# Preparing the split weights of later stages during the feed-forward stages of a ten-stage transformer kernel

## The chip, the core and the metric

The kernel runs on one NeuronCore of a Trainium2 chip. Its time is the device time of one execution in microseconds, from three executions. A profiled execution gives the trace that is read here. The engines are TensorE (PE in the views, and PEld for its weight loads), VectorE (DVE), ScalarE (ACT), GpSimd (POOL) and SyncE (SP), whose queue issues all of this kernel's DMAs.

## The reference, cut to what matters

Two hybrid layers (each: feed-forward, mix, feed-forward) and one block of four branches with a last feed-forward follow each other, on 512 tokens of width 1024, in float32.

```python
def hybrid_layer(x, pos, ...):                      # twice, l = 0 and 1
    x = x + 0.5 * swiglu(rmsnorm(x, ffn1_norm), ffn1_w_gate, ffn1_w_up, ffn1_w_down)
    h = rmsnorm(x, mix_norm) @ w_in                 # the mix stage: three kinds of attention
    ...
    x = x + jnp.concatenate([o_a, o_b, o_c], axis=-1) @ w_out
    x = x + 0.5 * swiglu(rmsnorm(x, ffn2_norm), ffn2_w_gate, ffn2_w_up, ffn2_w_down)

# second_block: four branches of h = rms(x), each gated and projected
y_fox = _merge_heads(_fox_attention(fq, fk, fv, log_f))      # "fox"
y_lru = _rg_lru_branch(proj("lru_x"), proj("lru_g"), ...)    # the recurrence, "lru"
y_sb  = _merge_heads(_stick_breaking_attention(sq, sk, sv))  # stick-breaking, "sb"
y_mem = _merge_heads(_mem_attention(mq, mk, mv))             # "mem"
...
x = x + (jax.nn.silu(gate_pre) * val) @ w_down[l]            # the last feed-forward
```

## The kernel before

The stages run one after the other: ffn(1,0), mix 0, ffn(2,0), ffn(1,1), mix 1, ffn(2,1), mem, fox, lru, sb, the output projection, and the last feed-forward (`ffn2`). In `ffn(f, l)` f is 1 or 2 and l the layer.

Every product of float32 numbers is made of three matmuls on halves (`mm3`, lines 308 to 310): each operand is held as a rounded part and a remainder. For a weight the two parts are made on the chip when it is needed, by `weights`: a DMA brings the raw weight (`raw`, 2 buffers; line 289), ACT copies it into the rounded part (`wh`, 4 buffers; line 293), and the remainder (`wl`, 4 buffers) is subtracted on line 296, by DVE for one weight and by POOL for the next:

```python
WENG = ("av", "ap")
raw = self.wp.tile([P, 1024], FT, name="raw", bufs=2)
hi, sub = WENG[self.wc % len(WENG)]
self.wc += 1
(nc.vector if sub == "v" else nc.gpsimd).tensor_sub(lo[:, :n], raw[:, :n], h[:, :n].bitcast(FT))
```

There are two `raw` buffers and two entries in `WENG`, and both are taken in turn by the same calls, so one buffer's weights always go to DVE and the other's to POOL.

A feed-forward has two halves, of 12 and 10 hidden tiles. For each tile a gate and an up weight (512 KB each) give 24 matmuls apiece (`pd` and `pa`); sigmoid on ACT, products on DVE and POOL (line 408) and a split follow. Then eight down steps, each of two weights: 384 KB and 18 matmuls apiece in the first half ("down of 12"), 320 KB and 15 apiece in the second ("down of 10"), and DVE adds the result to `x` (line 420).

The mix stages, fox and sb are written as plans of steps (projections, heads); the tile framework's scheduler then orders the instructions of each engine, once, when the program is built. Each engine executes its list in that order, and so does SP with the DMAs: what stands behind a waiting instruction waits as well.

Of the kernel before, what the change touches and what calls it, by code (L numbers as in the profile page):

```python
# [17 lines left out]
FT = mybir.dt.float32  # L18
# [179 lines left out]
class Build:  # L198
    def __init__(self, ctx, tc, I):
        self.tc, self.nc, self.I = tc, tc.nc, I  # L200
        nc = self.nc
        e = ctx.enter_context
        self.hlp = e(tc.tile_pool(name="hlp", bufs=1))
        self.wp = e(tc.tile_pool(name="wp", bufs=3))
        self.xp = e(tc.tile_pool(name="xp", bufs=1))
        self.fp = e(tc.tile_pool(name="fp", bufs=7))
        self.sp = e(tc.tile_pool(name="sp", bufs=2))
        self.cp = e(tc.tile_pool(name="cp", bufs=1))
        self.np_ = e(tc.tile_pool(name="np_", bufs=1))
# [12 lines left out]
        self.spare = True  # L222

    def consts(self):
        nc = self.nc
# [54 lines left out]
                self.early.append(self.weights(first.pop(0), D))  # L280


    def weights(self, ap, n):

        nc = self.nc
        raw = self.wp.tile([P, 1024], FT, name="raw", bufs=2)
        h = self.wp.tile([P, 1024], FR, name="wh", bufs=4)
        lo = self.wp.tile([P, 1024], FR, name="wl", bufs=4)
        nc.sync.dma_start(raw[:, :n], ap)
        hi, sub = WENG[self.wc % len(WENG)]  # L290
        self.wc += 1
# [99 lines left out]

    def ffn(self, f, l):
        nc, I = self.nc, self.I
        hs, rb, _ = self.norm(f"ffn{f}_{l}")
        for half, (a, b) in enumerate(HALVES):
            hid = []
            for n in range(a, b):
                wg = self.early.pop(0) if self.early else self.weights(I[f"wg{f}_{l}"][n], D)
                pg = self.ps()
                self.proj(pg, wg, hs)  # L400
                wu = self.early.pop(0) if self.early else self.weights(I[f"wu{f}_{l}"][n], D)
                pu = self.ps("pa")
# [12 lines left out]
            for n in range(KD):
                po = self.ps()
                for q in range(2):
                    w = self.weights(wd[2 * n + q], kg * P)
                    self.proj(po, w, hid[q * kg:(q + 1) * kg], start=q == 0, stop=q == 1)
                nc.vector.scalar_tensor_tensor(self.x[n], po, 0.5, self.x[n], op0=OP.mult, op1=OP.add)  # L420


    def halves(self, src, scale=None):
# [170 lines left out]
    def mix(self, l):  # L594
        nc, I = self.nc, self.I
        hs, rb, rc = self.norm(f"mix_{l}", spill=True)
        ci, si, tk = (self.table(k) for k in (2, 3, 4))
        win = I[f"win_{l}"]

        def tile_of(n):  # L600
            w = self.weights(win[n], D)
            ps = self.ps()
            self.proj(ps, w, hs)
            return ps
# [91 lines left out]
            ckv.append(rkc)  # L696

        def values_a():
            wa = [self.weights(I[f"wav_{l}"][g], 768) for g in range(4)]
            va.extend(self.hl("v") for _ in range(3))  # L700
            self.tokens(hs, wa, 384, 2, 384, lambda t, p: self.values(p, va, t, rc[:, t:t + 1], A_H))

        def values_b():
            wb = [self.weights(I[f"wbv_{l}"][g], 640) for g in range(4)]
            vb.extend(self.hl("v") for _ in range(3))
            self.tokens(hs, wb, 320, 2, 320, lambda t, p: self.values(p, vb, t, rc[:, t:t + 1], B_H))

        def values_c():
            wv = self.weights(I[f"wuv_{l}"], 640)
# [14 lines left out]
        def dense_c(h):  # L724
            p, s = divmod(h, 2)
            if p not in kn:
                m = P if p < 2 else 64
                wkn = self.weights(I[f"wuk_{l}"][p], 256)
# [8 lines left out]
            w = self.weights(I[f"wuq_{l}"][h], 384)  # L737
            pq = self.ps()
            self.proj(pq, w, cq)
            f, g = self.f(), self.f("g")  # L740
# [159 lines left out]
        return self.stack_k(self.halves(f), tags=("qk", "e"))  # L900

    def vgroup(self, hs, name, grp, rc):
        w = [self.weights(self.I[name][2 * grp + q], 1024) for q in range(2)]
# [54 lines left out]
    def fox(self, hs, rb, rc):  # L958
# [2 lines left out]
        vs, qs, ks, ys, got = {}, {}, {}, [], []  # L961

        def forget(_):
            w = self.weights(I["w2ff"], P)
# [23 lines left out]
            vs[2 * g], vs[2 * g + 1] = self.vgroup(hs, "w2fv", g, rc)  # L988

        def queries(p):  # L990
            w = self.weights(I["w2fq"][p], D)
            ps = self.ps()
            self.proj(ps, w, hs)
            qs[p] = self.qnorm(ps, self.g("fqg"))

        def keys(p):
            w = self.weights(I["w2fk"][p], D)
# [35 lines left out]

    def lru(self, hs, rb, rc):
        nc, I = self.nc, self.I
        wa = self.weights(I["w2la_"], D)
        wx = self.weights(I["w2lx_"], D)
        ys = []
        for d0 in range(0, KD, 2):
            xcs = self.sp.tile([P, 1280], FT, name="st")  # L1040
            gates = []
            for e in range(2):
                d = d0 + e
                w = self.weights(I["w2lx"][d], D)
# [24 lines left out]
            self.gate(1, d0, hs, rb, "g")  # L1069
            us = []  # L1070
            for d, xc, r, i, a, th in gates:
                w = self.weights(I["w2lg"][d], D)
                pg = self.ps()
                self.proj(pg, w, hs)
                u, v = self.f(), self.f("fa")
# [16 lines left out]
    def sb(self, hs, rb, rc):  # L1092
# [5 lines left out]
            vs[2 * g], vs[2 * g + 1] = self.vgroup(hs, "w2sv", g, rc)  # L1098

        def queries(p):  # L1100
            w = self.weights(I["w2sq"][p], D)
            ps = self.ps()
            self.proj(ps, w, hs)
            f = self.f()
# [1 line left out]
            qs[p] = self.stack_q(self.halves(f))  # L1106

        def keys(p):
            w = self.weights(I["w2sk"][p], D)
            ps = self.ps()  # L1110
            self.proj(ps, w, hs)
            f = self.f()
# [174 lines left out]
    def ffn2(self):  # L1287
# [60 lines left out]
```

## Time and profile before

| | us |
|---|---|
| median of 3 executions (lowest, highest) | 3549.71 (3545.65, 3551.51) |
| profiled execution, its time | 3547.53 |
| its span, first to last instruction | 3545.1 |
| PE busy in it | 3452.3 |
| ACT, POOL, DVE busy | 1432.8, 1534.5, 1959.9 |
| mean granted clock of TensorE | 0.988 |

The profiled execution's time is 2.4 us more than its span, and 2.2 us below the median. Busy time of PE is the union of pipelined matmuls: where it is the whole of a stretch, matmuls follow each other without a gap.

### The profile page before, as it was taken

The page shows a single profiled execution, that of the slowest core. Times are in us where ns is not written, and L with a number is a line of the kernel's source. Part 1 is how long each engine was busy: PE and PEld are TensorE (multiplying, and loading weights), DVE is VectorE, ACT ScalarE, POOL GpSimd, SP SyncE. Part 2 cuts the span into 40 slices and gives each one's busy share as a digit, 9 for nine tenths or more (in the row PEclk, how much of TensorE's full clock was granted, in tenths as well). Part 3 has the DMA queues.
Part 4 walks back from the last instruction along what each step waited for, and adds up shares of the span by engine and source line. Part 5 has one row for each costly group of instructions (what it writes and reads, how often), then busy time and mean ns, then how long its engine had stood idle before and what let it go on. Part 6 is the DMA issues. An engine that isn't in the chain of part 4 may idle for free.

```text
span 3545.1 us, 45441 instructions
## 1 busy us (share of the span) xinstructions
PE 3452.3 (97%) x16648; PEld 2882.8 (81%) x16648; DVE 1959.9 (55%) x3210; ACT 1432.8 (40%) x2366; POOL 1534.5 (43%) x1224
## 2 busy tenths in 40 slices
PE   8999999999999999999999999999999999999999
PEld 7888778788888888777888888888777788888887
DVE  5434697653445344796643465358536655657363
ACT  4223455532333233465422344346525445533222
POOL 3333346342424232446333343258635557635342
PEclk9999999999999999999999999999999999999999
DMA  3333433333233333334433243344532454442332
GB/s 134 91 106 107 128 99 112 109 99 97 94 98 95 95 101 124 110 90 118 122 93 108 85 129 107 104 132 137 152 122 90 157 160 129 128 143 95 95 101 89
DMA packets 141261, 397.60 MB, mean 112 GB/s; under 512 B 18144, under 2 KB 21600, under 8 KB 141040
## 3 DMA queue, kind: packets, MB, share of 16 engines
q1 hardware_dynamic: 141040, 394.71, 36.6%
q8 instruction: 132, 2.16, 0.3%
q14 instruction: 89, 0.73, 0.1%
HBM read 327.24 MB, written 20.48 MB: 98 GB/s over the span
## 4 chain that ended last, share of the span: by engine, by line
PE 47%; DVE 5%; POOL 2%; ACT 2%; issue 2%; DMA 1%; SPq 0%; POOLq 0%; ACTq 0%; DVEq 0%
PE pd L308 10%; PE pd L309 10%; PE pd L310 10%; PE pa L308 4%; PE pa L309 4%; PE pa L310 4%; PE po L527 1%; PE pt L517 1%; DVE wl L296 1%; PE pa L456 1%; POOL st L503 0%; DMA qk<-nt 0%; DVE st L1087 0%; POOL f L499 0%; ACT wh L293 0%
## 5 line engine op out<-in xcount | busy, mean ns | idle before, releaser
L296 POOL TENSOR_TENSOR wl<-raw,wh 128x1024 fp32r<-128x1024 f32 (+3 forms) x315 | 718.0, 2279 | 1135.7 <-ACT wh L293 1112.7
L293 ACT ACTIVATE wh<-raw 128x1024 fp32r<-128x1024 f32 (+3 forms) x631 | 609.5, 967 | 1323.7 <-PE pd L309 841.2
L308 PE MATMUL pd<-hs,wh 128*128 128x512 f32 (+1 forms) x2008 | 791.2, 395 | 19.7 <-ACT wh L293 7.8
L309 PE MATMUL pd<-hs,wh 128*128 128x512 f32 (+1 forms) x2008 | 790.9, 394 | 5.8 <-DVE hs L303 5.4
L310 PE MATMUL pd<-hs,wl 128*128 128x512 f32 (+1 forms) x2008 | 790.5, 394 | 2.4 <-DVE wl L296 1.7
L296 DVE TENSOR_TENSOR wl<-raw,wh 128x1024 fp32r<-128x1024 f32 (+3 forms) x316 | 383.4, 1213 | 232.8 <-ACT wh L293 226.2
L308 PEld LDWEIGHTS pd<-hs,wh 128*128 128x128 f32 (+1 forms) x2008 | 378.4, 189 | 100.7 <-ACT wh L293 14.1
L309 PEld LDWEIGHTS pd<-hs,wh 128*128 128x128 f32 (+1 forms) x2008 | 379.2, 189 | 84.8 <-DVE hs L303 6.2
L310 PEld LDWEIGHTS pd<-hs,wl 128*128 128x128 f32 (+1 forms) x2008 | 378.6, 189 | 85.2 <-DVE wl L296 4.6
L308 PE MATMUL pa<-hs,wh 128*128 128x512 f32 x896 | 349.3, 390 | 0.0
L309 PE MATMUL pa<-hs,wh 128*128 128x512 f32 x896 | 349.2, 390 | 0.0
L310 PE MATMUL pa<-hs,wl 128*128 128x512 f32 x896 | 349.0, 389 | 0.0
L408 POOL TENSOR_TENSOR f<-f,g 128x512 f32<-128x512 f32 x88 | 145.0, 1650 | 279.9 <-ACT g L406 273.5
L407 DVE TENSOR_TENSOR f<-pa,rb 128x512 f32<-128x512 f32 x88 | 60.8, 691 | 272.4 <-PE pa L310 272.4
L310 PEld LDWEIGHTS pa<-hs,wl 128*128 128x128 f32 x896 | 168.4, 188 | 35.0
L309 PEld LDWEIGHTS pa<-hs,wh 128*128 128x128 f32 x896 | 168.2, 188 | 34.9
L308 PEld LDWEIGHTS pa<-hs,wh 128*128 128x128 f32 x896 | 168.4, 188 | 34.6
L480 POOL TENSOR_SCALAR st<-st,ta 128x128 f32<-128x128 f32 x192 | 111.7, 584 | 107.1 <-DVE ta L479 101.0
L303 DVE TENSOR_TENSOR pt<-pt 128x384 fp32r<-128x384 f32 (+1 forms) x200 | 116.8, 597 | 50.0 <-ACT pt L302 48.7
L308 PE MATMUL pd<-ys,wh 128*128 128x512 f32 x362 | 142.3, 393 | 0.2 <-DVE f L741 0.2
L310 PE MATMUL pd<-ys,wl 128*128 128x512 f32 x362 | 141.9, 392 | 0.0
L309 PE MATMUL pd<-ys,wh 128*128 128x512 f32 x362 | 141.8, 392 | 0.0
(385 smaller groups left out, 6468.3 us busy)
## 6 DMA issues: line engine op xcount, KB each, us to landing
raw<-in_wg_dram SPq DMA_DIRECT2D x88, 512.0 KB, 3.5
raw<-in_wu_dram SPq DMA_DIRECT2D x88, 512.0 KB, 3.4
raw<-in_win_dram SPq DMA_DIRECT2D x38, 512.0 KB, 3.5
qk<-nt SPq DMA_DIRECT2D x76, 256.0 KB, 3.9
raw<-in_w2gt_dram SPq DMA_DIRECT2D x32, 512.0 KB, 3.7
raw<-in_w2br_dram SPq DMA_DIRECT2D x32, 512.0 KB, 3.5
qk<-nt SPq DMA_DIRECT2D x108, 128.0 KB, 2.5
raw<-in_wd1a_dram SPq DMA_DIRECT2D x32, 384.0 KB, 3.0
```

The source lines that it names most:

```text
L293: nc.scalar.activation(h[:, :n], raw[:, :n], AF.Copy)
L296: (nc.vector if sub == "v" else nc.gpsimd).tensor_sub(lo[:, :n], raw[:, :n], h[:, :n].bitcast(FT))
L303: (eng or nc.vector).tensor_sub(dst[rows, 1, cols], src, dst[rows, 0, cols].bitcast(FT))
L308: mm(out, wh, xh, start=start, stop=False)
L309: mm(out, wh, xl, start=False, stop=False)
L310: mm(out, wl, xh, start=False, stop=stop)
L407: nc.vector.tensor_mul(u, pu, rb)
L408: nc.gpsimd.tensor_mul(ga, ga, s)
L456: self.nc.tensor.matmul(ps[:, :n], q[:, s, t], k[s][:, x, :n], start=x == 0, stop=x == 1)
L480: nc.gpsimd.tensor_scalar(st[:, c], st[:, c], sm, 0.0, op0=OP.mult, op1=OP.add)
L517: nc.tensor.transpose(pt[:, at + (i - lo) * P:at + (i - lo + 1) * P], st[:, OFF[i] + j * P:OFF[i] + (j + 1) * P], self.ident)
L527: nc.tensor.matmul(po[:, q:q + n], va[:, o:o + P], w[:, x, c:c + n], start=j == 0 and x == 0, stop=j == 2 * g + 1 and x == 1)
```

## The change

The weights of mix 0 are loaded and split during ffn(1,0), those of mix 1 during ffn(2,0), those of fox (and two of the recurrence) during ffn(1,1), and those of the recurrence and of sb during ffn(2,1). `prepare` does it: a raw load and a split like any other, in the same buffers and with the same turn of DVE and POOL, and then two DMAs that store `wh` and `wl` in DRAM tiles. When the later stage asks for such a weight, two DMAs bring the two parts back into `wh` and `wl`, and no raw load, copy or subtraction is made. The gate and branch weights of block 2, `wo`, `w2o`, and all of mem stay as they were.

Per mix stage 36 weights are prepared (19 of 512 KB, 4 of 384, 5 of 320, 5 of 192, 3 of 128), 27 in ffn(1,1) (26 of 512 KB and one of 64) and 40 in ffn(2,1), all of 512 KB. They are spread evenly over 35 steps of a feed-forward: all hidden tiles but the first three, and the 16 down steps.

```diff
-    def weights(self, ap, n):
+    def weights(self, ap, n, key=None):
         nc = self.nc
+        if key in self.ahead:
+            t = self.ahead.pop(key)
+            h = self.wp.tile([P, 1024], FR, name="wh", bufs=4)
+            lo = self.wp.tile([P, 1024], FR, name="wl", bufs=4)
+            nc.sync.dma_start(h[:, :n].bitcast(FT), t[0])
+            nc.sync.dma_start(lo[:, :n].bitcast(FT), t[1])
+            return h, lo
...
+    def prepare(self, share):
+        self.due += share
+        while self.due >= 1 and self.todo:
+            self.due -= 1
+            name, n, *idx = self.todo.pop(0)
+            h, lo = self.w(name, n, *idx)
+            t = self.dp.tile([2, P, n], FT, name=f"ah_{name}_{'_'.join(map(str, idx))}")
+            self.nc.sync.dma_start(t[0], h[:, :n].bitcast(FT))
+            self.nc.sync.dma_start(t[1], lo[:, :n].bitcast(FT))
+            self.ahead[name, *idx] = t
...
     def ffn(self, f, l):
+        self.todo, self.due = AHEAD.get((f, l), [])[:], 0.0
+        share = len(self.todo) / (NF + 2 * KD - 3)
...
                 hid.append(t)
+                if n > 2:
+                    self.prepare(share)
...
                 nc.vector.scalar_tensor_tensor(self.x[n], po, 0.5, self.x[n], op0=OP.mult, op1=OP.add)
+                self.prepare(share)
+        self.prepare(len(self.todo) + 1)
...
+    for l, at in ((0, (1, 0)), (1, (2, 0))):
+        out[at] = ([(f"win_{l}", D, n) for n in range(19)] + [(f"wav_{l}", 768, g) for g in range(4)]
+                   + [(f"wbv_{l}", 640, g) for g in range(4)] + [(f"wuv_{l}", 640)]
+                   + [(f"wuk_{l}", 256, p) for p in range(3)] + [(f"wuq_{l}", 384, h) for h in range(C_H)])
+    out[1, 1] = ([("w2ff", P)] + [(f"w2f{n}", D, p) for n in "qkv" for p in range(8)] + [("w2la_", D), ("w2lx_", D)])
+    out[2, 1] = [(f"w2l{n}", D, d) for n in "xg" for d in range(8)] + [(f"w2s{n}", D, p) for n in "qkv" for p in range(8)]
```

Three places in the order that the scheduler made. The first is SP in ffn(1,0), from the last gate and up weights of the first half into its down steps. Before:

```order
L289 DMA raw<-in_wg_0_dram 128x1024
L289 DMA raw<-in_wu_0_dram 128x1024
L289 DMA raw<-in_wd1a_dram 128x768 x16
L289 DMA raw<-in_wg_0_dram 128x1024
L289 DMA raw<-in_wu_0_dram 128x1024
```

The same place in the changed program, where `ah_` tiles are those in DRAM:

```order
L297 DMA raw<-in_wd1a_dram 128x768
L297 DMA raw<-in_win_dram 128x1024
L297 DMA raw<-in_wd1a_dram 128x768
L321 DMA ah_win_9_1199<-wh 128x1024
L322 DMA ah_win_9_1199<-wl 128x1024
L297 DMA raw<-in_wd1a_dram 128x768
L297 DMA raw<-in_win_dram 128x1024
L297 DMA raw<-in_wd1a_dram 128x768
L321 DMA ah_win_10_1258<-wh 128x1024
L322 DMA ah_win_10_1258<-wl 128x1024
```

Between two pairs of down weights there is now one raw load of a mix weight, and its two stores stand ahead of the second down weight's load, which takes the buffer that this mix weight leaves.

The second place is POOL's list there, before:

```order
L296 TENSOR_TENSOR wl<-raw,wh 128x1024
L408 TENSOR_TENSOR f<-f,g 128x512
L296 TENSOR_TENSOR wl<-raw,wh 128x768
L408 TENSOR_TENSOR f<-f,g 128x512
L296 TENSOR_TENSOR wl<-raw,wh 128x768 x7
L296 TENSOR_TENSOR wl<-raw,wh 128x1024 x2
L408 TENSOR_TENSOR f<-f,g 128x512
```

And in the changed program:

```order
L304 TENSOR_TENSOR wl<-raw,wh 128x768
L304 TENSOR_TENSOR wl<-raw,wh 128x1024
L436 TENSOR_TENSOR f<-f,g 128x512
L304 TENSOR_TENSOR wl<-raw,wh 128x768 x2
L304 TENSOR_TENSOR wl<-raw,wh 128x1024
L304 TENSOR_TENSOR wl<-raw,wh 128x768 x2
L304 TENSOR_TENSOR wl<-raw,wh 128x1024
L304 TENSOR_TENSOR wl<-raw,wh 128x768 x2
L304 TENSOR_TENSOR wl<-raw,wh 128x1024
L304 TENSOR_TENSOR wl<-raw,wh 128x768
```

Every third subtraction that POOL makes in these steps is now one of a 512 KB mix weight.

The third place is SP at the start of fox, whose DMAs `qk<-nt`, `e<-nt` and `x<-dc` place queries, keys and decays for its heads. Before:

```order
L289 DMA raw<-in_w2fq_dram 128x1024
L289 DMA raw<-in_w2fk_dram 128x1024
L289 DMA raw<-in_w2fv_dram 128x1024 x2
L449 DMA qk<-nt 64x1024 x2
L449 DMA e<-nt 64x1024 x2
L440 DMA qk<-nt 64x512 x4
```

And in the changed program:

```order
L291 DMA wh<-ah_w2fk_10347 128x1024
L481 DMA qk<-nt 64x1024 x2
L481 DMA e<-nt 64x1024 x2
L291 DMA wh<-ah_w2fv_11126 128x1024
L292 DMA wl<-ah_w2fv_11126 128x1024
L472 DMA qk<-nt 64x512 x4
L291 DMA wh<-ah_w2fv_11252 128x1024
L292 DMA wl<-ah_w2fv_11252 128x1024
```

Each weight is two loads instead of one here, and each waits for a `wh` or `wl` buffer that a projection has read, where before it waited for a `raw` buffer.

## Rows read from the trace of the kernel before

**Rows 1.** The page, part 1: busy us, share of the span, instructions.

```profile
PE 3452.3 (97%) x16648; PEld 2882.8 (81%) x16648; DVE 1959.9 (55%) x3210; ACT 1432.8 (40%) x2366; POOL 1534.5 (43%) x1224
```

**Rows 2.** Windows by stage: busy us of each engine, granted clock, DMA share, GB/s.

```profile
374.00:684.00 310.00, 291.45 (x1522) 242.82 (x1521) 241.78 (x581) 165.31 (x357) 148.29 (x140) 0.96 0.39 111
684.00:1052.00 368.00, 368.00 (x1631) 304.92 (x1630) 167.50 (x173) 115.71 (x148) 123.77 (x61) 1.00 0.31 96
...
1417.00:1717.00 300.00, 281.04 (x1488) 233.44 (x1488) 229.46 (x579) 164.06 (x354) 144.10 (x139) 0.97 0.40 111
1717.00:2083.00 366.00, 366.00 (x1627) 303.36 (x1626) 170.09 (x177) 120.88 (x160) 140.42 (x72) 1.00 0.33 99
...
2290.00:2620.00 330.00, 315.49 (x1818) 272.26 (x1817) 186.94 (x552) 169.92 (x327) 193.95 (x242) 0.97 0.47 139
2620.00:2830.00 210.00, 198.91 (x842) 159.71 (x841) 133.30 (x131) 101.18 (x129) 109.36 (x64) 0.98 0.35 116
2830.00:3130.00 300.00, 290.80 (x1647) 251.88 (x1646) 172.34 (x228) 153.17 (x306) 195.33 (x238) 0.99 0.50 146
```

**Rows 3.** Timeline of DVE, down steps of 12 in ffn(2,0).

```profile
853.22 0.69 DVE L420 SCALAR_TENSOR_TENSOR x<-pd,x 128x512 f32<-128x512 f32 x1 [2.47 <-PE pd L310]
...
861.38 0.69 DVE L420 SCALAR_TENSOR_TENSOR x<-pd,x 128x512 f32<-128x512 f32 x1 [2.47 <-PE pd L310]
```

**Rows 4.** Groups by form in 684 to 1052 (ffn(2,0)): xcount, busy us, mean ns.

```profile
L296 POOL TENSOR_TENSOR wl<-raw,wh 128x1024 fp32r<-128x1024 f32 x22 | 58.7, 2670 | 78.2 <-ACT wh L293 78.2
L293 ACT ACTIVATE wh<-raw 128x1024 fp32r<-128x1024 f32 x45 | 47.8, 1061 | 144.7 <-PE pd L309 75.4 <-PE pa L309 60.8 <-DMA raw<-in_wu_dram 4.4
...
L296 POOL TENSOR_TENSOR wl<-raw,wh 128x768 fp32r<-128x768 f32 x8 | 14.7, 1837 | 44.7 <-ACT wh L293 44.7
...
L293 ACT ACTIVATE wh<-raw 128x768 fp32r<-128x768 f32 x16 | 13.6, 847 | 47.9 <-PE pd L309 40.1 <-PE pa L309 7.7
L296 POOL TENSOR_TENSOR wl<-raw,wh 128x640 fp32r<-128x640 f32 x8 | 13.0, 1622 | 38.3 <-ACT wh L293 38.3
...
L293 ACT ACTIVATE wh<-raw 128x640 fp32r<-128x640 f32 x16 | 11.8, 739 | 36.3 <-PE pd L309 28.2 <-PE pa L310 4.1 <-PE pa L309 3.8
```

**Rows 5.** DMA issues in 684 to 1052: count, KB each, median us to landing.

```profile
raw<-in_wg_dram SPq DMA_DIRECT2D x23, 512.0 KB, 3.3
...
raw<-in_wd2a_dram SPq DMA_DIRECT2D x16, 384.0 KB, 3.1
raw<-in_wd2b_dram SPq DMA_DIRECT2D x16, 320.0 KB, 2.9
```

**Rows 6.** Timeline of all engines in fox, one raw buffer from issue to issue.

```profile
2385.92 0.81 SPq L289 DMA_DIRECT2D raw<-in_w2fv_dram  x2
...
2390.79 2.39 POOL L296 TENSOR_TENSOR wl<-raw,wh 128x1024 fp32r<-128x1024 f32 x1
...
2393.20 0.33 SPq L289 DMA_DIRECT2D raw<-in_w2fq_dram  x1
```

**Rows 7.** DMA view of 2824 to 2846, at the start of sb.

```profile
DMA packets 2552, 5.96 MB, mean 271 GB/s; under 512 B 282, under 2 KB 282, under 8 KB 2551
...
raw<-in_w2sq_dram SPq DMA_DIRECT2D x2, 512.0 KB, 4.3
...
raw<-in_w2sk_dram SPq DMA_DIRECT2D x2, 512.0 KB, 5.3
```

**Rows 8.** Longest wait of ACT in fox (2290 to 2620): total us, times, longest.

```profile
ACT wh L293 <- PE pd L309: 37.7, 14, 4.5
```

**Rows 9.** Longest wait of PE in fox, columns as in rows 8.

```profile
PE pa L456 <- DVE ta L473: 8.0, 5, 3.3
```

**Rows 10.** Windows at the ends of mix 0, mix 1 and fox, columns as in rows 2.

```profile
1650.00:1662.00 12.00, 6.78 (x27) 5.28 (x27) 6.42 (x18) 5.56 (x15) 11.92 (x13) 0.57 0.61 156
2556.00:2573.00 17.00, 9.64 (x33) 7.21 (x34) 9.33 (x35) 10.11 (x22) 9.51 (x18) 0.60 0.35 97
603.00:634.00 31.00, 22.33 (x102) 17.99 (x101) 25.35 (x60) 16.28 (x43) 23.03 (x25) 0.78 0.45 112
```

More of the change, by code (lines that the diff above doesn't have):

```diff
@@ L222, in __init__ @@
         self.spare = True
+        self.ahead, self.todo, self.due = {}, [], 0.0
     def consts(self):
@@ L297, in weights, with w @@
         return h, lo
+    def w(self, name, n, *idx):
+        ap = self.I[name]
+        for i in idx:
+            ap = ap[i]
+        return self.weights(ap, n, (name, *idx))
+    def prepare(self, share):
[8 more added lines that the diff above has]
+            self.ahead[name, *idx] = t
     def split(self, dst, src, rows=slice(0, P), cols=slice(0, S), eng=None):
@@ L597, in mix @@
         ci, si, tk = (self.table(k) for k in (2, 3, 4))
-        win = I[f"win_{l}"]
         def tile_of(n):
-            w = self.weights(win[n], D)
+            w = self.w(f"win_{l}", D, n)
             ps = self.ps()
@@ L698, in values_a @@
         def values_a():
-            wa = [self.weights(I[f"wav_{l}"][g], 768) for g in range(4)]
+            wa = [self.w(f"wav_{l}", 768, g) for g in range(4)]
             va.extend(self.hl("v") for _ in range(3))
@@ L703, in values_b @@
         def values_b():
-            wb = [self.weights(I[f"wbv_{l}"][g], 640) for g in range(4)]
+            wb = [self.w(f"wbv_{l}", 640, g) for g in range(4)]
             vb.extend(self.hl("v") for _ in range(3))
@@ L708, in values_c @@
         def values_c():
-            wv = self.weights(I[f"wuv_{l}"], 640)
+            wv = self.w(f"wuv_{l}", 640)
             vc.extend((self.hl("v"), self.hl("e"), self.hl("e")))
@@ L727, in dense_c @@
                 m = P if p < 2 else 64
-                wkn = self.weights(I[f"wuk_{l}"][p], 256)
+                wkn = self.w(f"wuk_{l}", 256, p)
                 kn[p] = self.ps()
@@ L736, in dense_c @@
             self.split(k, f[0:96], rows=slice(0, 96), eng=nc.gpsimd)
-            w = self.weights(I[f"wuq_{l}"][h], 384)
+            w = self.w(f"wuq_{l}", 384, h)
             pq = self.ps()
@@ L902, in vgroup @@
     def vgroup(self, hs, name, grp, rc):
-        w = [self.weights(self.I[name][2 * grp + q], 1024) for q in range(2)]
+        w = [self.w(name, 1024, 2 * grp + q) for q in range(2)]
         vs = [self.hl("v") for _ in range(2)]
@@ L963, in forget @@
         def forget(_):
-            w = self.weights(I["w2ff"], P)
+            w = self.w("w2ff", P)
             pf = self.ps()
@@ L990, in queries @@
         def queries(p):
-            w = self.weights(I["w2fq"][p], D)
+            w = self.w("w2fq", D, p)
             ps = self.ps()
@@ L996, in keys @@
         def keys(p):
-            w = self.weights(I["w2fk"][p], D)
+            w = self.w("w2fk", D, p)
             ps = self.ps()
@@ L1035, in lru @@
         nc, I = self.nc, self.I
-        wa = self.weights(I["w2la_"], D)
-        wx = self.weights(I["w2lx_"], D)
+        wa = self.w("w2la_", D)
+        wx = self.w("w2lx_", D)
         ys = []
@@ L1043, in lru @@
                 d = d0 + e
-                w = self.weights(I["w2lx"][d], D)
+                w = self.w("w2lx", D, d)
                 px = self.ps()
@@ L1071, in lru @@
             for d, xc, r, i, a, th in gates:
-                w = self.weights(I["w2lg"][d], D)
+                w = self.w("w2lg", D, d)
                 pg = self.ps()
@@ L1100, in queries @@
         def queries(p):
-            w = self.weights(I["w2sq"][p], D)
+            w = self.w("w2sq", D, p)
             ps = self.ps()
@@ L1108, in keys @@
         def keys(p):
-            w = self.weights(I["w2sk"][p], D)
+            w = self.w("w2sk", D, p)
             ps = self.ps()
@@ L1316, in ffn2, with _ahead @@
                 nc.vector.tensor_add(self.x[n], self.x[n], po)
+def _ahead():
+    out = {}
+    for l, at in ((0, (1, 0)), (1, (2, 0))):
[4 more added lines that the diff above has]
+    out[2, 1] = [(f"w2l{n}", D, d) for n in "xg" for d in range(8)] + [(f"w2s{n}", D, p) for n in "qkv" for p in range(8)]
+    return out
+AHEAD = _ahead()
 FULL = (("ffn", 1, 0), ("mix", 0), ("ffn", 2, 0), ("ffn", 1, 1), ("mix", 1), ("ffn", 2, 1), ("block2", "mem,fox,lru,sb", True),
```

## The prediction

> **What bounds the kernel now.** I read the page first: PE is busy for 3452.3 us, 97% of the span [rows 1], so at most 93 us of waiting and whatever the clock costs can be won back. Then the windows by stage [rows 2]: in ffn(2,0) and ffn(2,1) PE is busy for every microsecond (368.00 of 368.00, 366.00 of 366.00) at full clock, while ACT is busy for a third of the time, POOL for 34 to 38% and DVE for under half. The feed-forwards that take the work over are bound by PE alone. The five stages that give it away are not: PE idles for 18.6 us in mix 0, 19.0 in mix 1, 14.5 in fox, 11.1 in the recurrence and 9.2 in sb, together 72.3 us. Their clock is below 1.00, and at 0.96, 0.97, 0.97, 0.98 and 0.99 another 12.4 + 9.0 + 9.9 + 4.2 + 3.0 = 38.5 us go to the lower level of 1.2 GHz. Together 110.8 us is all that the change can win.
>
> So two questions decide: how much of the 110.8 us hangs on weights, and whether the feed-forwards can supply more weights than PE eats without PE waiting. Busy shares answer the second wrongly; it is a question of latency in a ring of two buffers.
>
> **What PE asks for.** A down step of 12 takes 861.38 - 853.22 = 8.16 us [rows 3] for 36 matmuls, 0.2267 us each. A down step of 10 (30 matmuls) so takes 6.80 us, a gate and up step (48 matmuls) 10.88 us.
>
> **What the ring of `raw` gives.** A weight holds its buffer from the issue of its load until its subtraction ends, because the next load waits for that. In fox one such turn lies bare: the load is issued at 2385.92, POOL subtracts from 2390.79 for 2.39 us, and the buffer's next load goes out at 2393.20, 7.28 us after the first and 0.02 us after POOL [rows 6]. The parts in a feed-forward: the load lands in 3.3 us for 512 KB, 3.1 for 384, 2.9 for 320 [rows 5]; ACT copies in 1.06, 0.85 and 0.74; POOL subtracts in 2.67, 1.84 and 1.62 [rows 4]. Hand-overs I put at 0.14 us. A turn through POOL is then 7.17, 5.93 and 5.40 us. DVE's turns are shorter, but weights alternate strictly between the two buffers, so the buffer whose weights go to POOL sets the pace: a step's weights take half the sum of their POOL turns. In the kernel before a down step of 12 takes (5.93 + 5.93) / 2 = 5.93 us of the 8.16, and ACT idles until PE frees a slot [rows 4]. With prepared weights:
>
> - ffn(1,0) and ffn(2,0), 36/35 = 1.03 a step. Gate and up with 512 KB: 3.03 x 7.17 / 2 = 10.86 against 10.88. Down of 12: (11.86 + 1.03 x 7.17) / 2 = 9.62 against 8.16, 1.46 us lost a step. Down of 10, where the prepared weights are small (one of 320 KB, three of 128 and five of 192, which I put at 3.6 and 4.2 us on a line through the turns of 512 and 320): (16 x 5.40 + 37.2) / 16 = 7.73 against 6.80, 0.93 lost. Over 8 steps each, 11.7 + 7.4 = 19 us.
> - ffn(1,1), 0.77 a step: gate and up 9.93, nothing lost; down of 12 8.69, of 10 8.16: 4.2 + 10.9 = 15 us.
> - ffn(2,1), 1.14 a step: gate and up 11.26, 0.38 lost in 19 steps; down of 12 10.02, of 10 9.49: 7.2 + 14.9 + 21.5 = 44 us.
>
> Four slots of `wh` let supply run ahead of PE before a stretch that is short of it: two down weights (8.16 us) less a copy and a subtraction (2.7), some 5 us. I take 5 off for each separate stretch: two in each of the first three stages, one in ffn(2,1), where no step is free to recover. That leaves 9 + 9 + 5 + 39 = 62 us, the low bound.
>
> **The landing under more traffic.** The two stores are 1 MB, and SP places the second just ahead of a raw load. the 14.2 MB of a mix stage, loaded once and stored twice over, are 42.6 MB more in 365 us and bring ffn(1,0) and ffn(2,0) from about 100 to about 215 GB/s, ffn(1,1) the same, and the 63 MB of 40 weights bring ffn(2,1) to 271 if it is not stretched. At 271 GB/s 512 KB loads landed in 4.3 and 5.3 us [rows 7], against 3.3 at 96 GB/s [rows 2, 5]. Each 1 us more adds half of it per weight of a step. The lower bound is 0 more, the upper 1.0 in every turn. I take 0.2 for three stages, nearer the light end since queues are mostly empty at 215, and 0.5 for ffn(2,1), which slows its own traffic. The same sums: ffn(1,0) 3.1 (11 steps at 11.16) + 14.1 + 9.9 - 10 = 17, ffn(2,0) 17, ffn(1,1) 6.5 + 13.1 - 10 = 10, ffn(2,1) 22.2 + 21.2 + 27.8 - 5 = 66: together 110 us. At 1.0 they are 60, 60, 36 and 94, 250 us.
>
> The Trainium skill speaks of this landing too: "DMA: Bandwidth & Descriptors", section "Latency and other measured facts", gives an HBM access latency of 0.2 us on average and 2 us at high load. By it a turn could grow by 1.8 us, and my sum for the feed-forwards would be some 400 us instead of 110. The rows above agree that load lengthens the landing, but by 1 to 2 us at 271 GB/s only.
>
> **What the five stages win.** Per 512 KB weight ACT is spared 1.06 us, POOL 2.4 or DVE 1.2. No wait of PE in fox names a weight; the longest is for the softmax on DVE [rows 9]. The gain is indirect: ACT stands 37.7 us in fox with a weight's copy at the head of its list, waiting for a `wh` slot that PE frees [rows 8], and exponentials stand behind it. That wait goes, for ACT and for what POOL and DVE do after it. SP takes it over: the loads into `wh` and `wl` wait for the same slots, and key and query DMAs stand behind them. What weights cannot touch are the ends of stages, where the last head drains: in the three windows of rows 10 PE idles 8.7 + 5.2 + 7.4 us, and their clocks cost 6.8 + 5.2 + 6.8: 40 us. Of the other 71 us I take half, 35, with 0 and 71 as bounds; one queue is freed and another loaded, so neither end has the better claim. In these stages 512 KB more per weight and 0.33 us more of SP's issue lie beside PE.
>
> **The sum.** 3547.5 + 110 - 35 = 3622 us, 75 us slower than the profiled execution, which is 2 us below the median of the three runs; the result is read against that. About 0.2% (7 us) is what a measurement of this kernel can tell from no change.
>
> **The rivals.**
> 1. *Faster: the freed queues win.* In fox and the mix stages ACT's list no longer stands for weights, the whole 71 us come back, and only ffn(2,1), where even gate and up steps lack supply, loses its 39: 3547.5 - 71 + 39 = 3516. For it: the waits of rows 8, and three of the feed-forwards are short of supply in down steps alone. Against: their deficits of 0.5 to 1.5 us a step are sums without any wait in them. It decides where the feed-forwards lose less than the stages win.
> 2. *About even.* The low bound of 62 against a gain of 62: 3548.
> 3. *The clock falls in the feed-forwards.* PE would stand for 1 to 3.5 us in each down step. In 603 to 634 it idled for 8.7 us and the granted clock was 0.78, so another 6.8 us went [rows 10]: 0.78 us for each idle one. On 110 us that is 86: 3622 + 86 = 3708. Against: part of the slower matmuls falls into waits that are there anyway. The Trainium skill, "TensorE: Matmul & The Clock Gate", section "HAM oscillation — how this bites in real kernels", describes this: a kernel whose matmuls wait for the next weights is throttled at every tile. The mix stages' rows agree, at 0.96 and 0.97, and no feed-forward here shows it.
> 4. *Traffic.* Every turn is 1 us longer: 3547.5 + 250 - 35 = 3762. Against: the slower stage moves its bytes more slowly.
> 5. *The change does nothing* is excluded: the lists of SP and POOL differ as shown. That the supply is hidden everywhere is rival 1 taken further.
>
> **How the numbers follow.** Forecast 0.66, rival 1 0.13, rival 2 0.08, rival 3 0.06, rival 4 0.07. So faster by over 0.2% 0.13, within it 0.08, slower 0.79. The prediction is 3622. Under the forecast alone the time runs from 3574 (the low bound of 62, the gain of 35) to 3686 (17 + 17 + 10 + 94 = 138, the last at 1.0 us more, and no gain). The range reaches to the even case below and just past the clock case above, 3540 to 3715; outside are rival 1, most of which is below, and rival 4.
>
> **What would show it.** Right: in the changed trace ffn(2,1) is the longest, some 430 us, the others 375 to 385, with PE idle in their down steps and ACT's copies there waiting for the landing of `raw` instead of for PE; POOL turns of 7 to 8 us without a pause; PE's idle time in fox and the mix stages smaller by about a third, their ends unchanged; the last feed-forward as before. Wrong: PE unbroken in the down steps, which would mean that a buffer's turn is shorter than its parts; or landings of 5 us; or mix and fox longer, with SP standing at a load into `wh` while a head waits for its keys.

## The result

The changed kernel takes 3729.65 us (median of four runs, 3723.32 to 3735.36) against 3550.24 for the kernel before: a ratio of 1.0509, interval 1.0492 to 1.0526. The forecast of slower was right; the size was not: 180 us where 75 were forecast, 15 us beyond the range. The profiled execution took 3723.32 us, its span is 3721.6.

Part 1 of the page after, which answers to [rows 1]: PE is busy for 59 us longer, with as many matmuls, and its share has fallen from 97% to 94%.

```profile
PE 3511.4 (94%) x16648; PEld 2896.5 (78%) x16648; DVE 1885.9 (51%) x3210; ACT 1447.5 (39%) x2369; POOL 1479.7 (40%) x1224
```

The windows after, first the four feed-forwards in their order, then mix 0, mix 1, fox, the recurrence and stick-breaking (columns as in [rows 2]):

```profile
36.00:418.00 382.00, 352.17 (x1488) 282.35 (x1488) 156.31 (x169) 128.62 (x163) 139.08 (x75) 0.97 0.60 200
749.00:1134.00 385.00, 353.25 (x1506) 283.73 (x1504) 159.03 (x169) 129.52 (x165) 139.72 (x75) 0.98 0.59 195
1156.00:1525.00 369.00, 350.29 (x1502) 282.93 (x1500) 159.93 (x163) 125.14 (x154) 137.84 (x70) 0.99 0.59 201
1858.00:2268.00 410.00, 365.62 (x1506) 287.19 (x1505) 165.16 (x178) 146.78 (x180) 167.30 (x88) 0.96 0.66 226
...
418.00:748.00 330.00, 312.17 (x1631) 261.07 (x1632) 225.03 (x586) 152.91 (x338) 118.20 (x126) 0.97 0.52 161
1525.00:1858.00 333.00, 316.86 (x1637) 263.80 (x1638) 229.04 (x584) 153.58 (x340) 123.01 (x128) 0.97 0.53 162
2498.00:2828.00 330.00, 314.90 (x1821) 271.46 (x1820) 167.75 (x540) 148.50 (x303) 159.63 (x231) 0.97 0.60 179
2828.00:3018.00 190.00, 184.91 (x795) 149.81 (x794) 112.14 (x119) 89.18 (x115) 83.78 (x55) 0.98 0.51 174
3018.00:3300.00 282.00, 279.06 (x1614) 245.08 (x1613) 157.71 (x211) 126.15 (x277) 159.02 (x225) 0.99 0.62 190
```

PE, which had no gap in ffn(2,0) and ffn(2,1) [rows 2], now idles for 19 to 44 us in each feed-forward, at twice the traffic of before (96 to 104 GB/s there). Fox still has 15 us of idle time and 0.97.

Lengths of stages below are worked out from the traces: a feed-forward runs from DVE's first product of a gate to its last addition into `x`, a mix stage from there to the next first gate, and the three later stages between the last sigmoids of their gates on ACT. Before and after, in us: ffn(1,0) 338.4 and 382.3, ffn(2,0) 341.2 and 385.9, ffn(1,1) 343.3 and 369.8, ffn(2,1) 343.3 and 410.4, together +182; mix 0 334.0 and 330.6, mix 1 329.2 and 333.2, fox 330.9 and 330.2, the recurrence 203.8 and 190.0, stick-breaking 288.9 and 283.0, together -20; everything else, above all the memory stage, 692 and 706, +14. The memory stage's own work is that of before; why it is some 10 us longer stays open.

Within the feed-forwards the lengths can be split once more: the down steps, from the first to the last addition of each half, lose 116 us over the four stages (414.5 before, 530.8 after), and the rest, which is the gate and up steps with the first down step of each half, loses 66.

**Where a down step waits.** ACT's waits in the down steps of 12 of ffn(2,0), 881 to 951 (total us, times, longest):

```profile
ACT wh L301 <- DMA raw<-in_wd2a_dram: 33.4, 11, 6.2
ACT wh L301 <- DMA raw<-in_win_dram: 11.4, 6, 3.4
ACT wh L301 <- DMA raw<-in_wg_dram: 5.5, 1, 5.5
ACT wh L301 <- DMA ah_win<-wh: 4.1, 1, 4.1
```

Before, the same copy waited there for PE to free a slot (40.1 of 47.9 us, [rows 4]); now for the landing of `raw`, for PE never. One turn lies bare in the timeline (start, duration):

```profile
900.64 0.33 SPq L321 DMA_DIRECT2D ah_win<-wh  x1
...
901.06 0.38 SPq L297 DMA_DIRECT2D raw<-in_wd2a_dram  x1
...
906.35 0.84 ACT L301 ACTIVATE wh<-raw 128x768 fp32r<-128x768 f32 x1 [5.74 <-DMA raw<-in_wd2a_dram]
907.27 1.82 POOL L304 TENSOR_TENSOR wl<-raw,wh 128x768 fp32r<-128x768 f32 x1 [6.26 <-ACT wh L301]
...
909.12 0.33 SPq L297 DMA_DIRECT2D raw<-in_win_dram  x1
```

The load is issued 0.42 us behind a store, ACT starts 5.29 us later, and copy and subtraction take what they took before. The buffer's next load goes out 8.06 us after the first; I had 5.93. This turn is a long one. Over the seven steps from the first to the last addition (DVE's timeline) a step takes (951.17 - 880.90) / 7 = 10.04 us, against 8.16 before [rows 3]:

```profile
880.90 0.68 DVE L450 SCALAR_TENSOR_TENSOR x<-pd,x 128x512 f32<-128x512 f32 x1
...
951.17 0.69 DVE L450 SCALAR_TENSOR_TENSOR x<-pd,x 128x512 f32<-128x512 f32 x1 [4.57 <-PE pd L336]
```

The DMA view of ffn(2,0) after (749 to 1134: count, KB each, median us to landing; [rows 5] before: 3.3, 3.1 and 2.9):

```profile
DMA packets 25585, 75.15 MB, mean 195 GB/s; under 512 B 2832, under 2 KB 5904, under 8 KB 25567
...
raw<-in_win_dram SPq DMA_DIRECT2D x19, 512.0 KB, 3.6
raw<-in_wg_dram SPq DMA_DIRECT2D x19, 512.0 KB, 4.2
...
ah_win<-wl SPq DMA_DIRECT2D x19, 512.0 KB, 3.5
raw<-in_wu_dram SPq DMA_DIRECT2D x19, 512.0 KB, 4.8
raw<-in_wd2a_dram SPq DMA_DIRECT2D x16, 384.0 KB, 4.0
raw<-in_wd2b_dram SPq DMA_DIRECT2D x16, 320.0 KB, 3.3
```

The loads that suffer most are those right behind a store. Over the four feed-forwards, 512 KB loads issued within 0.6 us of a store landed in 4.8 us (median of 87), the others in 3.9 (181).

So the suspects are the ring of two `raw` buffers, the landing under the stores' traffic, and the clock, which fell to 0.96 to 0.99.

### The profile page after: what moved, and what is told of

Same layout as the page of the kernel before. It is cut to its first block, busy times and chain, and to the rows that moved or that the text cites. A ratio compares the mean times of both kernels' runs of the same rounds, so it can differ in the third digit from the quotient of the medians.

```text
span 3721.6 us, 46418 instructions
## 1 busy us (share of the span) xinstructions
PE 3511.4 (94%) x16648; PEld 2896.5 (78%) x16648; DVE 1885.9 (51%) x3210; ACT 1447.5 (39%) x2369; POOL 1479.7 (40%) x1224
## 5 line engine op out<-in xcount | busy, mean ns | idle before, releaser
L304 POOL TENSOR_TENSOR wl<-raw,wh 128x1024 fp32r<-128x1024 f32 (+3 forms) x315 | 691.3, 2195 | 1279.6 <-ACT wh L301 1196.8
L304 DVE TENSOR_TENSOR wl<-raw,wh 128x1024 fp32r<-128x1024 f32 (+3 forms) x316 | 403.5, 1277 | 652.3 <-ACT wh L301 616.7
L436 POOL TENSOR_TENSOR f<-f,g 128x512 f32<-128x512 f32 x88 | 133.1, 1515 | 95.9 <-ACT g L434 91.2
L334 PE MATMUL pd<-ys,wh 128*128 128x512 f32 x362 | 147.4, 407 | 22.9 <-ACT wh L301 22.6
L335 PE MATMUL pd<-ys,wh 128*128 128x512 f32 x362 | 145.3, 402 | 0.0
L328 ACT ACTIVATE pt<-pt 128x384 fp32r<-128x384 f32 (+1 forms) x200 | 101.5, 527 | 95.6 <-PE pt L549 88.4
```

The source lines that it names most:

```text
L328: nc.scalar.activation(dst[rows, 0, cols], src, AF.Copy)
L334: mm(out, wh, xh, start=start, stop=False)
L335: mm(out, wh, xl, start=False, stop=False)
```

## The experiments

Each was compared with the kernel before on the same chip (medians 3546.8 to 3547.6). In the table, FFN is the sum of the four feed-forwards, "mix" of both mix stages, "later" of fox, the recurrence and stick-breaking; the last column is the rest of the span. These four columns are of the one profiled execution, the times and ratios of all.

| kernel | time, us | ratio to before (interval) | FFN | mix | later | rest |
|---|---|---|---|---|---|---|
| before | 3550.24 | | 1366 | 663 | 824 | 692 |
| after | 3729.65 | 1.0509 (1.0492 to 1.0526) | 1548 | 664 | 803 | 706 |
| all on DVE | 3586.28 | 1.0106 (1.0085 to 1.0127) | 1418 | 659 | 810 | 699 |
| three `raw` | 3603.18 | 1.0158 (1.0143 to 1.0173) | 1415 | 668 | 810 | 708 |
| no stores | 3626.13 | 1.0223 (1.0206 to 1.0240) | 1425 | 680 | 827 | 693 |
| stores alone | 3547.94 | 1.0008 (0.9998 to 1.0017) | 1366 | 665 | 826 | 693 |
| load first | 3723.74 | 1.0496 (1.0477 to 1.0515) | 1553 | 657 | 804 | 708 |
| gate steps only | 3536.46 | 0.9967 (0.9954 to 0.9980) | 1365 | 664 | 813 | 693 |
| free weights | 3500.08, one run | | 1368 | 641 | 792 | 698 |
| filled waits | 3751.64 | 1.0584 (1.0563 to 1.0605) | 1570 | 673 | 802 | 705 |
| recurrence only | 3543.67 | 0.9989 (0.9981 to 0.9998) | 1365 | 664 | 818 | 693 |

### A shorter turn: every subtraction on DVE

```diff
-WENG = ("av", "ap")
+WENG = ("av", "av")
```

> Every subtraction of a weight goes to VectorE; everything else is the changed kernel. Theory R (the ring of two raw buffers, each turn = landing + copy + subtraction): a turn through the buffer that went to GpSimd gets shorter by 1.18 us for 512 KB (2.40 to 1.22) and 0.88 us for 384 KB (1.84 to 0.96), so a down step of 12 with one prepared weight loses (0.88 + 0.88 + 1.18) / 2 = 1.5 us: 10.4 to about 8.9 us in ffn(1,0), 10.8 to 9.3 in ffn(2,1). Summed over the four feed-forwards about 95 us come back of the 182: 3635 us (3600 to 3665). Theory T (the traffic: the memory or the DMA engines deliver no faster, whoever subtracts): the landings grow by what the subtractions save, down steps stay at 10.0 to 10.8 us, 3710 to 3735 us.

Measured: 3586.28 us. 143 us come back, more than the 95 expected: the feed-forwards lose 52 us where they lost 182. There are as many bytes in fewer microseconds (220, 219, 216 and 246 GB/s where it was 200, 195, 201 and 226), so it is not a rate at which the memory stops. The last of these windows:

```profile
1752.00:2129.00 377.00, 355.95 (x1505) 283.94 (x1503) 198.03 (x232) 145.09 (x179) 48.76 (x33) 0.97 0.71 246
```

The 95 are what 1.5 us make in 64 down steps. The down steps gave 65 us back (they lose 52 where they lost 116), and the gate and up steps, which that sum left out, gave back all the 66 us that they had lost. DVE's subtractions also got shorter. Here they are in ffn(2,0) after, with POOL's:

```profile
L304 POOL TENSOR_TENSOR wl<-raw,wh 128x1024 fp32r<-128x1024 f32 x28 | 67.1, 2395 | 125.9 <-ACT wh L301 114.5 <-DMA raw<-in_wd2a_dram 4.8 <-DMA raw<-in_wu_dram 4.6
...
L304 DVE TENSOR_TENSOR wl<-raw,wh 128x1024 fp32r<-128x1024 f32 x29 | 41.5, 1432 | 81.8 <-ACT wh L301 76.4 <-DMA ah_wbv<-wl 5.4
...
L304 DVE TENSOR_TENSOR wl<-raw,wh 128x768 fp32r<-128x768 f32 x10 | 13.3, 1331 | 42.8 <-ACT wh L301 42.8
```

and in this kernel:

```profile
L304 DVE TENSOR_TENSOR wl<-raw,wh 128x1024 fp32r<-128x1024 f32 x58 | 71.0, 1225 | 81.5 <-ACT wh L301 48.0 <-DMA ah_win<-wl 24.9 <-DMA ah_wbv<-wl 8.2
L304 DVE TENSOR_TENSOR wl<-raw,wh 128x768 fp32r<-128x768 f32 x20 | 19.1, 956 | 32.1 <-ACT wh L301 25.9 <-DMA ah_win<-wl 6.2
```

Beside POOL's subtractions DVE's own took 0.2 to 0.4 us longer. The landings of DVE's buffer got shorter as well in that stage (mean 4.2 to 3.6 us). How much of the 143 us each of these two gave was not separated from POOL's longer subtraction.

### A third buffer

```diff
-SLOTS = {..., "nt": 2}
+SLOTS = {..., "nt": 1}
...
-        raw = self.wp.tile([P, 1024], FT, name="raw", bufs=2)
+        raw = self.wp.tile([P, 1024], FT, name="raw", bufs=3)
```

> The changed kernel with three raw buffers in place of two; the 4 KB a partition come from the second nt buffer, which the feed-forwards don't use and the mix stages do. Theory R: each buffer now has three weights' time for a turn, a down step of 12 needs about (6.5 + 6.5 + 7.7) / 3 = 6.9 us of supply against 8.16 of PE, and the feed-forwards' loss goes almost whole: 3550 to 3580 us, to which the mix stages may add up to 20 us for their lost buffer. Theory T: same bytes, same rate, down steps stay near 10 us, 3700 us or more.

Measured: 3603.18 us. Same bytes, and 126 us less: the traffic theory falls again. But 49 us of loss stay in the feed-forwards, and the expected 0 to 30 (3550 to 3580 us) was wrong. ACT's longest waits in ffn(2,1) (1890 to 2130), where 25 of the 49 lie, say why:

```profile
ACT wh L301 <- DMA ah_w2sk<-wh: 23.0, 8, 4.8
ACT wh L301 <- DMA ah_w2lg<-wh: 22.6, 5, 6.3
ACT wh L301 <- DMA raw<-in_w2sv_dram: 14.6, 5, 4.8
```

Now the copy waits for a store to finish reading its slot of `wh`. Behind the ring of two stands the ring of four: a prepared weight holds its slots until its stores have landed.

### The stores taken away, and the stores alone

Without stores: `prepare` loads and splits, then forgets.

```diff
             h, lo = self.w(name, n, *idx)
-            t = self.dp.tile([2, P, n], FT, name=f"ah_{name}_{'_'.join(map(str, idx))}")
-            self.nc.sync.dma_start(t[0], h[:, :n].bitcast(FT))
-            self.nc.sync.dma_start(t[1], lo[:, :n].bitcast(FT))
-            self.ahead[name, *idx] = t
```

> The feed-forwards load and split the extra weights but store nothing, and the later stages split their own weights as the kernel before does, so nothing is won there. Theory R, with the landing as the term that was too small: without the 1 MB of stores for each weight the landings fall back to 3.0 to 3.6 us, and the four feed-forwards lose the low bound of the prediction or a little more, 62 to 90 us: 3612 to 3640 us. Theory T (the stores' traffic is the cost): 3550 to 3570 us. If the stores cost nothing: 3730 us.

Stores alone: `prepare` stores the parts that the last call of `weights` returned.

```diff
-            h, lo = self.w(name, n, *idx)
+            h, lo, n = self.last
...
-            self.ahead[name, *idx] = t
```

> The feed-forwards split no extra weight; in its place they store the parts of the weight that PE is about to use (1 MB in a gate and up step, 0.77 or 0.64 MB in a down step), and the later stages split their own weights as before. Theory R: landings of 4 us or more behind the stores, but a down step of 12 has two turns of 5.93 + 1 on one buffer and so needs 6.9 us of 8.16: no loss in the feed-forwards, 3550 to 3570 us. Theory T: the stores are two thirds of the new bytes of these stages, so most of the 182 us stays: 3650 us or more.

Measured: 3626.13 and 3547.94 us. Without stores the four feed-forwards lose 9.3 + 12.2 + 8.6 + 28.5 = 58.6 us; the prediction's low bound, with no longer landing, was 9 + 9 + 5 + 39 = 62. All but 2 of the 58.6 lie in the down steps, and the clock stayed at 1.00 in all four stages. (The other 20 us of this kernel lie in mix 1, 16 us longer, and in the stages behind it; their work is that of before, and I have no cause for it.) DMA in its ffn(2,0):

```profile
DMA packets 15571, 47.32 MB, mean 134 GB/s; under 512 B 1728, under 2 KB 2752, under 8 KB 15552
...
raw<-in_wg_dram SPq DMA_DIRECT2D x20, 512.0 KB, 3.4
raw<-in_wu_dram SPq DMA_DIRECT2D x20, 512.0 KB, 3.3
...
raw<-in_wd2a_dram SPq DMA_DIRECT2D x16, 384.0 KB, 3.0
```

With the stores alone the same stage looks like this:

```profile
DMA packets 20740, 64.84 MB, mean 190 GB/s; under 512 B 2298, under 2 KB 2298, under 8 KB 20722
...
raw<-in_wu_dram SPq DMA_DIRECT2D x20, 512.0 KB, 4.2
raw<-in_wg_dram SPq DMA_DIRECT2D x20, 512.0 KB, 3.4
```

190 GB/s against 195 in the changed kernel, some landings nearly a microsecond longer, and no time is lost. Of two loads of 512 KB in one stage, `wu` lands in 4.2 us and `wg` in 3.4, and the timeline shows a store 0.38 us ahead of `wu`, while the next `wg` is issued 3.59 us behind that store:

```profile
871.83 0.33 SPq L323 DMA_DIRECT2D ah_win<-wl  x1
872.21 0.42 SPq L297 DMA_DIRECT2D raw<-in_wu_dram  x1
```

The two costs don't add: the ring alone costs 59 us, the stores alone nothing, both together 182. A longer landing costs only where the ring has no slack left.

### The order of store and load

Both stores of a weight wait in a list until two more raw loads are issued, so that the second store stands behind the load that waits for the same subtraction:

```diff
-            self.nc.sync.dma_start(t[0], h[:, :n].bitcast(FT))
-            self.nc.sync.dma_start(t[1], lo[:, :n].bitcast(FT))
+            self.pend.append([2, t, h, lo, n])
...
         nc.sync.dma_start(raw[:, :n], ap)
+        self.flush()
```

> The changed kernel with the second store of each prepared weight (its wl part) issued behind the raw load that waits for the same subtraction, no longer 0.4 us ahead of it; the first store goes out as soon as SyncE comes to it. Same bytes, same subtractions. Theory Q (a load pays for the store that stands just ahead of it): the loads that waited land in 3.5 to 3.8 us where they took 4.2 to 4.9, the 0.3 us of issue goes too, and with about half of the 123 us that the stores add to the ring's own 59 gone it gives 3660 to 3690 us. Theory T (the stores slow whatever is under way, in any order): the next load pays instead, 3715 to 3735 us.

Measured: 3723.74 us, 1.0496 of before where the change has 1.0509: the same. The theory that the loads get their time back once no store stands just ahead of them (Q) falls. In ffn(2,0) the price was only passed on:

```profile
raw<-in_wu_dram SPq DMA_DIRECT2D x19, 512.0 KB, 4.3
ah_win<-wl SPq DMA_DIRECT2D x19, 512.0 KB, 5.2
raw<-in_win_dram SPq DMA_DIRECT2D x18, 512.0 KB, 4.6
raw<-in_wd2a_dram SPq DMA_DIRECT2D x16, 384.0 KB, 3.6
```

`wu` lands in 4.3 where it took 4.8 and `wd2a` in 3.6 where it took 4.0, but `win` takes 4.6 where it took 3.6, and the store of `wl` 5.2 for 3.5. Over the four feed-forwards the mean landing of a 512 KB load is what it was (4.26 us, 4.24 in the changed kernel).

### The clock

```diff
                 for q in range(2):
+                    if w and not q:
+                        for _ in range(8):
+                            nc.tensor.matmul(po, w[0][:, :P], hid[-1][:, 0, :], start=True, stop=True)
                     w = self.weights(wd[2 * n + q], kg * P)
```

> The changed kernel with eight more matmuls (1.8 us of PE) ahead of each of 60 down steps, on the weight that PE holds already and into the bank that the step then starts anew: the result is the same, and PE works where it would wait for the next weight. Supply theory (the turn of raw sets a down step at 9.6 to 10.8 us for 12 and 7.8 to 10.2 for 10, and slower matmuls fit in it): the 109 us of added work vanish in the waits save some 13 us in the down steps of 10 of ffn(1,0) and ffn(2,0), where 6.80 + 1.8 exceeds 7.8: 3725 to 3750 us, at a granted clock of 0.99 or more in the feed-forwards. Clock theory (the prediction's third rival): the clock lost in these stages, 0.03 x 382 + 0.02 x 385 + 0.01 x 369 + 0.04 x 410 = 39 us, comes back: 3680 to 3700 us. If PE set the pace of the down steps: 3835 us.

Measured: 3751.64 us, 22 more than the changed kernel. The first step of each half has no weight before it, so 56 steps were filled, not 60, with 56 x 8 x 0.2267 = 102 us; 80 of them vanished in the waits. ffn(1,1) shows it best: PE is now busy almost throughout, at a full clock, and the stage is as long as in the changed kernel (368.8 us, 369.8 there), where PE was busy for 350.29 us at 0.99:

```profile
1156.00:1525.00 369.00, 368.11 (x1627) 304.29 (x1628) 156.03 (x168) 125.37 (x153) 137.31 (x72) 1.00 0.59 197
```

So the supply sets the pace there, not PE. That slower matmuls in those waits cost as little is an inference. In the other three stages the clock that I meant to restore stayed where it was (0.97, 0.98 and 0.96), so what a full clock would give was not measured; that this much work fits in only bounds it.

### What the receiving stages could win

One pair of parts, split once, serves every weight that the change prepares. The parts take the place of one slot, so `wh` and `wl` have three slots here and not four:

```diff
-        return self.weights(ap, n, (name, *idx))
+        if self.one is None:
+            h, lo = self.weights(ap, D)
+            self.one = [self.wp.tile([P, 1024], FR, name=k, bufs=1) for k in ("oh", "ol")]
+            self.nc.scalar.activation(self.one[0], h.bitcast(FT), AF.Copy)
+            self.nc.scalar.activation(self.one[1], lo.bitcast(FT), AF.Copy)
+        return self.one
```

> Every weight that the change prepares is replaced by one fixed pair of parts that lies in SBUF, so that these stages load and split none of them (their sums are of other weights); nothing is prepared, and wh and wl have three slots in place of four. It shows all that any supply of these weights can win: stage lengths count, not the total. Theory A (the prediction's: half of the idle time hangs on weights): mix and fox shorten by 8 to 15 us each, the recurrence and stick-breaking by more than the 14 and 6 of the changed kernel. Theory B (these stages wait for heads, softmax and normalisation, not for weights): mix and fox stay within 3 us of 334, 329 and 331 us, and only the recurrence and stick-breaking shorten.

Measured by stage: mix 0 334.0 to 324.6, mix 1 329.2 to 316.2, fox 330.9 to 327.7, the recurrence 203.8 to 178.8, stick-breaking 288.9 to 285.4: -54 us in all. The mix stages go with theory A, fox with B. Stick-breaking gains 3.5 us, less than the 5.9 of the changed kernel, which neither theory had; with three slots and another order this kernel, of which there is one execution, is not a strict upper bound. With free weights only the recurrence gets rid of its idle time; its window, against 0.98 before:

```profile
2613.00:2792.00 179.00, 178.02 (x786) 147.07 (x785) 105.41 (x118) 85.00 (x112) 78.26 (x53) 1.00 0.24 83
```

### Only where there is slack

```diff
-        share = len(self.todo) / (NF + 2 * KD - 3)
+        share = len(self.todo) / (NF - 3)
...
-                self.prepare(share)
         self.prepare(len(self.todo) + 1)
...
+    every = [("w2la_", D), ("w2lx_", D)] + [(f"w2l{n}", D, d) for d in range(8) for n in "xg"] + [(f"w2s{n}", D, p) for p in range(8) for n in "qkv"]
+    out = {at: every[k::4] for k, at in enumerate(((1, 0), (2, 0), (1, 1), (2, 1)))}
```

The `prepare` that goes is the one in the down steps, and these lists take the place of the change's.

> Only the weights of the recurrence and of stick-breaking (42 in place of 140) are prepared, and only in gate and up steps, 10 or 11 in each of the four feed-forwards; the mix stages and fox split their own as before. Ring theory: a gate and up step with 0.55 prepared weights needs (2.55 x 8.4) / 2 = 10.7 us at landings of 4.5 us against 10.88 of PE, so the feed-forwards lose 0 to 10 us; the recurrence gains the 14 us and stick-breaking the 6 us that they gained in the changed kernel: 3527 to 3545 us, faster than the kernel before. Rival: any prepared weight costs the feed-forwards its share of the 182 us (182 / 140 x 42 = 55 us): 3585 us.

Without the 24 weights of stick-breaking:

> As the kernel with 42 weights in gate and up steps, but only the 18 of the recurrence. There the recurrence gained 12 us, stick-breaking 2 us, and fox and the stretch ahead of it lost 7. If the losses come from the reloads of stick-breaking or are chance of the order: 3530 to 3540 us, the same as with 42. If stick-breaking's weights are worth their 2 us and no more: 3538 us.

Measured: 3536.46 and 3543.67 us. With 42 weights the kernel is faster than the kernel before, by 0.33% (0.9954 to 0.9980), and so faster than the changed one. The feed-forwards lose nothing: 1365 against 1366, with PE unbroken in the last of them:

```profile
1739.00:2082.00 343.00, 343.00 (x1516) 284.03 (x1515) 144.16 (x159) 118.05 (x152) 129.65 (x72) 1.00 0.43 142
```

The recurrence has 191.7 us and stick-breaking 286.6, where they had 203.8 and 288.9; with 18 weights 192.5 and 291.8. Fox is 3 to 4 us longer in both, although its own work is unchanged, and whether that is the order of instructions was not tried. The 3543.67 us lie outside what was expected for 18 weights (3530 to 3540): leaving out stick-breaking's weights cost 7 us where they had seemed worth 2, and 5 of them lie in stick-breaking itself.

## Why the prediction was right, and where it failed

Of the 105 us by which the forecast was short, the feed-forwards are 72 (182 where 110 were forecast), the gain in five stages 15, and the other stages, which the sum put at nothing, 14; the few that are left lie between the profiled executions, which these lengths are read from, and the medians.

- **The ring: right in its mechanism.** The turn, its parts and strict alternation gave 62 us without traffic; without stores 58.6 were measured, stage by stage 9.3, 12.2, 8.6 and 28.5 against 9, 9, 5 and 39. A shorter turn and a third buffer each gave most of the loss back. That ACT would wait for `raw` and no longer for PE, and that ffn(2,1) would be the longest, came as said (410.4; forecast 430). That the total came so near is partly luck: the sum took POOL's subtraction of 512 KB at the 2.67 us of before [rows 4], and it took 2.40 in the changed kernel. With 2.40 the 39 become 29, as measured, and the total falls below 50.
- **The landing under more traffic: this step failed.** The prediction put +0.2 us on a turn in three stages and +0.5 in ffn(2,1), "nearer the light end since queues are mostly empty at 215". No run shows them so: the DMA engines were busy for 0.59 to 0.66 of the time at 195 to 226 GB/s. From issue to issue, POOL's turns took 6.49, 6.51, 7.18 and 6.86 us without stores and 7.32, 7.23, 7.64 and 7.61 with them, stage by stage in order (means of 47 to 55 turns): +0.8, +0.7, +0.5 and +0.75, of which 0.5 to 0.7 are landing; SP's issue of a store ahead of the load takes 0.1 to 0.2. It shows most in the gate and up steps. The sum had their supply at 10.86 us of PE's 10.88 in ffn(1,0) and ffn(2,0), no slack at all, and forecast 28 us of loss in all four stages; 66 were measured. Redone step by step at +0.75 everywhere, the prediction's own sum gives some 185 us, about 60 of it in gate and up steps; 182 were measured. DVE's subtractions beside POOL's, up to 0.4 us longer, were in no term, and they and the 2.67 err in opposite directions.
- **The gain: mis-sized.** The prediction took 35 us of 71 in five stages, and 20 were measured, less 14 given back elsewhere. The recurrence (13.8; free weights give it 25) and stick-breaking (5.9) gained; mix and fox, from which most was to come, gave 0.1, and PE's idle time in mix 0, mix 1 and fox, forecast to shrink by a third, went from 18.6, 19.0 and 14.5 us to 17.8, 16.1 and 15.1. Free weights give mix 22 us and fox 3: in fox little hung on the supply of weights. As forecast, most of ACT's 37.7 us [rows 8] is gone (14.6 are left) and SP stands instead. Its waits in fox after:

```profile
SPq L291 <- PE pd L336: 45.4, 12, 7.9
```

  and what PE itself waits for longest in fox is what it was [rows 9]:

```profile
PE pa L488 <- DVE ta L505: 6.8, 4, 3.3
```

- **Rival 3, the clock:** it did fall, by some 39 us worth in the feed-forwards' windows (a granted clock of 0.96 to 0.99 where it was 1.00), but 80 of 102 us of added matmuls found room there: as the text against it said, slow matmuls fall into waits. So it looks like a symptom here; that some of the 182 us is its own is not excluded.
- **Rival 4, traffic,** with +1 us on every turn and 3762 us, was nearest in its number, and its mechanism was the missing term. It is no rate of the memory, though: as many stores cost nothing without the extra turns, and the kernel with all subtractions on DVE moved its bytes at a higher rate.
- **Rivals 1 and 2** fell with the change as it was made. In gate and up steps alone, and for the stages that gain, rival 1's sign comes true, at 11 us.

## What to carry to other kernels

Count an engine's slack in turns of the smallest ring that feeds it, not in busy shares: in the feed-forwards ACT, POOL and DVE were each idle for more than half the time, and two buffers were the limit. Price a load's landing in a run that has the stores, too: here it cost 0.5 to 0.7 us a turn, and issuing the load ahead of the store did not save it. Widen one ring only after asking which ring holds the same data next. Before work is moved to make a stage faster, give it that work for free once: some 54 us was all there was to win here.

## What the runs showed of the hardware

A 512 KB load that landed in 3.3 us before landed in 4.8 right behind one of the kernel's own stores and in 3.9 elsewhere in the feed-forwards (medians, at 195 to 226 GB/s); changing which transfer goes first only passed the delay on. And DVE and POOL subtractions hinder each other: in ffn(2,0) DVE's took 1.225 us for 512 KB and 0.956 for 384 KB when POOL subtracted nothing, 1.432 and 1.331 in the changed kernel beside it. In the timeline of the changed kernel one DVE subtraction of 384 KB meets POOL's:

```profile
913.92 2.40 POOL L304 TENSOR_TENSOR wl<-raw,wh 128x1024 fp32r<-128x1024 f32 x1 [4.84 <-DMA raw<-in_wd2a_dram]
...
915.37 1.77 DVE L304 TENSOR_TENSOR wl<-raw,wh 128x768 fp32r<-128x768 f32 x1 [4.43 <-ACT wh L301]
```

POOL ends at 916.32; from there to DVE's end at 917.14 are 0.82 us, near the 0.956 of one alone. The Trainium skill, "SBUF — State Buffer", section "SBUF: two separate sides", describes such a lock: a DVE operation with two inputs in SBUF and a GpSimd operation that reads SBUF exclude each other, and the later one waits. The trace agrees.

The same wait the other way round is in the kernel before, and in the forecast's 2.67 us with it: 66 of POOL's 219 subtractions of 512 KB began while DVE ran an operation on two operands in SBUF (`f<-f`). They took 2.78 us on average, and each ended 2.25 to 2.27 us after that operation did. The 79 that began while DVE was idle took 2.40. One of the 66:

```profile
745.21 0.69 DVE L409 TENSOR_TENSOR f<-f 128x512 f32<-128x512 f32 x1
745.38 2.79 POOL L296 TENSOR_TENSOR wl<-raw,wh 128x1024 fp32r<-128x1024 f32 x1 [3.12 <-ACT wh L293]
```

In the changed kernel only 4 of POOL's meet that operation.
